# A gather kernel: index work by single batches in three steps, with TensorE and VectorE in program order

## The chip, the cores and the metric

One core of a Trainium2 chip. Times are device microseconds (us) of a whole execution. The runs of a kernel spread by 0.5 to 5%: those of the kernel before lie between 89.6 and 94.3 us over all their runs (one outlier of 171.8 left out as slow). A run more than 1.5% over the fastest of its kernel in the same set of runs counts as slow.

## The reference

```python
batch, seq, dim = 32, 512, 1024              # x: 32 x 512 x 1024 float32, indices: 32 x 128
for b in range(batch):
    result[b] = x[b, indices[b]]             # 128 rows of 4 KB per batch
```

Some of the 128 indices of a batch repeat. The kernel fetches each distinct row once, into a ring buffer, and spreads it to its places with a product by a 0/1 matrix.

## The kernel before

`HEAD` = 3 batches are fetched plainly. For the other 29, index work ("prep") finds the first user of each row (`junk`, `cnt`, `lead`), ranks the leaders by a product (`sm`, then `nth`, `slot`), packs row numbers by a second product (`pack`, `sm`, then `at`, `atF`) and makes the spreading matrix `s`. It is done for groups of two and then four batches.

```python
def prep(g0, g1):                                   # one group of up to four batches
    n, w = g1 - g0, slice(g0, g1)
    bc = pbc.tile([N, 4, N], F32, name="bc")        # PSUM, 2 buffers
    for b in range(g0, g1): nc.tensor.matmul(bc[:, b - g0], ...)
    for b in range(g0, g1): nc.vector.scalar_tensor_tensor(out=junk[:], in0=bc[:, b - g0], ..., accum_out=cnt[:, b:b + 1])
    nc.vector.tensor_scalar(out=lead16[:, w], ...); nc.vector.tensor_scalar(out=lead[:, w], ...)
    sm = psm.tile([N, B], F32, name="sm")           # PSUM, 2 buffers
    nc.tensor.matmul(sm[:, :n], lhsT=above[:], rhs=lead16[:, w], ...)
    # nth <- sm, nth ^= shift, slot <- nth: one VectorE operation each for the group
    for b in range(g0, g1):
        # pack <- turn, slot, lead
        last = nc.tensor.matmul(sm[:, 4 + b - g0:5 + b - g0], lhsT=pack[:], rhs=near[:, b:b + 1], ...)
    # at <- sm, atF <- sm: one each for the group
    for b in range(g0, g1): nc.vector.tensor_scalar(out=s[:], in0=bc[:, b - g0], scalar1=atF[:, b:b + 1], ...)
    return last
# ... cut
for b in range(HEAD, B):
    while done < len(groups) and groups[done][0] <= b + AHEAD:   # AHEAD = 8
        last = prep(*groups[done]); done += 1
    u = held[(b - HEAD) % RING]                                  # RING = 8
    gather(u, at[:, b:b + 1], b, bounds_check=S - 1, oob_is_err=False)
    ps = pout.tile([N, D], F32, name="ps")                       # PSUM, 2 buffers
    with tc.issue_after(last.ins):
        for h in range(2): nc.tensor.matmul(ps[:, h * 512:(h + 1) * 512], lhsT=spread[b][:], rhs=u[...], ...)
    if b < HEAD + 10:
        nc.scalar.copy(out=blocks[b][:], in_=ps[:])
    else:
        nc.vector.tensor_copy(out=blocks[b][:, :512], in_=ps[:, :512])
        nc.scalar.copy(out=blocks[b][:, 512:], in_=ps[:, 512:])
    nc.sync.dma_start(out=of[b * N:(b + 1) * N], in_=blocks[b][:])
```

Of the kernel before, what the change touches and what calls it, by code (L numbers as in the profile page):

```python
# [6 lines left out]
F32 = mybir.dt.float32  # L7
F16 = mybir.dt.float16
I32 = mybir.dt.int32
ALU = mybir.AluOpType  # L10


@with_exitstack
def kernel(ctx, tc, x, indices, out):
# [8 lines left out]



    nc = tc.nc
    B, S, D = x.shape
    N = indices.shape[1]
    HEAD, RING, FAR, AHEAD = 3, 8, 1024, 8
    assert S <= FAR  # L30
    const = ctx.enter_context(tc.tile_pool(name="const", bufs=1))
    ring = ctx.enter_context(tc.tile_pool(name="ring", bufs=1))
    rows = ctx.enter_context(tc.tile_pool(name="rows", bufs=1))
    pick = ctx.enter_context(tc.tile_pool(name="pick", bufs=1))
    junkp = ctx.enter_context(tc.tile_pool(name="junk", bufs=4))
    PS = bass.MemoryType.PSUM
    pbc = ctx.enter_context(tc.tile_pool(name="pbc", bufs=2, space=PS))
    psm = ctx.enter_context(tc.tile_pool(name="psm", bufs=2, space=PS))
    pout = ctx.enter_context(tc.tile_pool(name="pout", bufs=2, space=PS))


    first = const.tile([N, 1], indices.dtype, name="first")
    nc.sync.dma_start(out=first[:], in_=indices.rearrange("b n -> n b")[:, 0:1])
    v = const.tile([B, N], indices.dtype, name="v")
    nc.sync.dma_start(out=v[:], in_=indices)

    def low(t):
        return t[:].bitcast(I32).rearrange("p (n two) -> p n two", two=2)[:, :, 0]


    diff = const.tile([N, N], I32, name="diff")
    nc.gpsimd.iota(diff[:], pattern=[[1, N]], base=0, channel_multiplier=-1)
    rank = const.tile([N, 16, 8], I32, name="rank")
    for e in range(16):
        fold = 0
        for bit, col in enumerate((7, 5, 6, 3)):
            fold ^= col * (e >> bit & 1)
        steps = [[(-16 if fold >> bit & 1 else 16) << bit, 2] for bit in (2, 1, 0)]
        nc.gpsimd.iota(rank[:, e], pattern=steps, base=e + 16 * fold, channel_multiplier=0)  # L59
    shift = const.tile([N, 2, 16], I32, name="shift")  # L60
    nc.gpsimd.iota(shift[:], pattern=[[0, 2], [1, 16]], base=0, channel_multiplier=0)

    zero = const.tile([N, 1], F32, name="zero")
    nc.vector.memset(zero[:], 0.0)
    ident = const.tile([B, B], F16, name="ident")
    nc.vector.tensor_scalar(out=ident[:], in0=diff[:B, :B], scalar1=0, scalar2=None, op0=ALU.is_equal)
    below = const.tile([N, N], F16, name="below")
    nc.vector.tensor_scalar(out=below[:], in0=diff[:], scalar1=0, scalar2=None, op0=ALU.is_lt)
    above = const.tile([N, N], F16, name="above")
    turn = const.tile([N, N], F16, name="turn")  # L70
    nc.vector.tensor_copy(out=turn[:], in_=rank[:].rearrange("p e q -> p (e q)"))
    masks = nc.vector.tensor_scalar(out=above[:], in0=diff[:], scalar1=0, scalar2=None, op0=ALU.is_gt)
    vf = const.tile([B, N], F16, name="vf")
    with tc.issue_after(masks.ins):
        nc.vector.tensor_copy(out=vf[:], in_=low(v))  # L75


    tr = psm.tile([N, B], F32, name="sm")
    nc.tensor.matmul(tr[:], lhsT=vf[:], rhs=ident[:], start=True, stop=True)  # L79
    idxT = const.tile([N, B], I32, name="idxT")  # L80
    nc.vector.tensor_copy(out=idxT[:], in_=tr[:])
    idxF = const.tile([N, B], F32, name="idxF")
    nc.vector.tensor_copy(out=idxF[:], in_=tr[:])
    near = const.tile([N, B], F16, name="near")
    nc.vector.tensor_scalar(out=near[:], in0=tr[:], scalar1=float(-FAR), scalar2=None, op0=ALU.add)

    xf = x.flatten_outer_dims()
    of = out.flatten_outer_dims()

    def gather(dst, at, b, **kw):  # L90
        nc.gpsimd.indirect_dma_start(  # L91
            out=dst[:], out_offset=None,
            in_=xf[:], in_offset=bass.IndirectOffsetOnAxis(ap=at, axis=0),
            element_offset=b * S * D, **kw)

    blocks = [rows.tile([N, D], F32, name=f"block{b}") for b in range(B)]
    for b in range(HEAD):
        gather(blocks[b], first[:].bitcast(I32)[:, 0:1] if b == 0 else idxT[:, b:b + 1], b)
        nc.sync.dma_start(out=of[b * N:(b + 1) * N], in_=blocks[b][:])

    cnt = const.tile([N, B], F32, name="cnt")
    lead = const.tile([N, B], F32, name="lead")
    lead16 = const.tile([N, B], F16, name="lead16")
    nth = const.tile([N, B], I32, name="nth")
    slot = const.tile([N, B], F32, name="slot")
    atF = const.tile([N, B], F32, name="atF")
    at = const.tile([N, B], I32, name="at")
    spread = {}

    def prep(g0, g1):  # L110
        n, w = g1 - g0, slice(g0, g1)
        bc = pbc.tile([N, 4, N], F32, name="bc")
        for b in range(g0, g1):
            nc.tensor.matmul(bc[:, b - g0], lhsT=ident[:, b:b + 1].to_broadcast([B, N]),  # L114
                             rhs=vf[:], start=True, stop=True)
        for b in range(g0, g1):
            junk = junkp.tile([N, N], F16, name="junk")
            nc.vector.scalar_tensor_tensor(  # L118
                out=junk[:], in0=bc[:, b - g0], scalar=idxF[:, b:b + 1],
                in1=below[:], op0=ALU.is_equal, op1=ALU.mult, accum_out=cnt[:, b:b + 1])  # L120
        nc.vector.tensor_scalar(out=lead16[:, w], in0=cnt[:, w], scalar1=0.0, scalar2=None, op0=ALU.is_equal)  # L121
        nc.vector.tensor_scalar(out=lead[:, w], in0=cnt[:, w], scalar1=0.0, scalar2=None, op0=ALU.is_equal)  # L122
        sm = psm.tile([N, B], F32, name="sm")
        nc.tensor.matmul(sm[:, :n], lhsT=above[:], rhs=lead16[:, w], start=True, stop=True)  # L124
        nc.vector.tensor_copy(out=nth[:, w], in_=sm[:, :n])  # L125
        nc.vector.tensor_tensor(out=nth[:, w], in0=nth[:, w],  # L126
                                in1=shift[:].rearrange("p t s -> p (t s)")[:, w], op=ALU.bitwise_xor)
        nc.vector.tensor_copy(out=slot[:, w], in_=nth[:, w])  # L128
        for b in range(g0, g1):
            pack = junkp.tile([N, N], F16, name="pack")  # L130
            nc.vector.tensor_scalar(out=pack[:], in0=turn[:], scalar1=slot[:, b:b + 1],  # L131
                                    scalar2=lead[:, b:b + 1], op0=ALU.is_equal, op1=ALU.mult)
            last = nc.tensor.matmul(sm[:, 4 + b - g0:5 + b - g0], lhsT=pack[:], rhs=near[:, b:b + 1],  # L133
                                    start=True, stop=True)
        nc.vector.tensor_scalar(out=at[:, w], in0=sm[:, 4:4 + n], scalar1=float(FAR), scalar2=None, op0=ALU.add)  # L135
        nc.vector.tensor_scalar(out=atF[:, w], in0=sm[:, 4:4 + n], scalar1=float(FAR), scalar2=None, op0=ALU.add)
        for b in range(g0, g1):
            s = pick.tile([N, N], F32, name=f"s{b}")
            nc.vector.tensor_scalar(out=s[:], in0=bc[:, b - g0], scalar1=atF[:, b:b + 1],  # L139
                                    scalar2=None, op0=ALU.is_equal)  # L140
            spread[b] = s
        return last

    held = []
    for k in range(RING):
        u = ring.tile([N, D], F32, name=f"u{k}")
        nc.scalar.copy(out=u[:], in_=zero[:].to_broadcast([N, D]))  # L147
        held.append(u)

    groups = [(HEAD, HEAD + 2)] + [(g, min(g + 4, B)) for g in range(HEAD + 2, B, 4)]  # L150
    done = 0
    for b in range(HEAD, B):
        while done < len(groups) and groups[done][0] <= b + AHEAD:
            last = prep(*groups[done])
            done += 1
        u = held[(b - HEAD) % RING]
        gather(u, at[:, b:b + 1], b, bounds_check=S - 1, oob_is_err=False)
        ps = pout.tile([N, D], F32, name="ps")
        with tc.issue_after(last.ins):
            for h in range(2):  # L160
                nc.tensor.matmul(ps[:, h * 512:(h + 1) * 512], lhsT=spread[b][:],  # L161
                                 rhs=u[:, h * 512:(h + 1) * 512], start=True, stop=True)
        if b < HEAD + 10:
            nc.scalar.copy(out=blocks[b][:], in_=ps[:])  # L164
        else:
            nc.vector.tensor_copy(out=blocks[b][:, :512], in_=ps[:, :512])  # L166
            nc.scalar.copy(out=blocks[b][:, 512:], in_=ps[:, 512:])  # L167
        nc.sync.dma_start(out=of[b * N:(b + 1) * N], in_=blocks[b][:])


# [28 lines left out]
```

## Time and profile before

| kernel before | |
|---|---|
| median of 3 runs at the time of the prediction | 93.65 us (92.63 to 94.29) |
| span of the profiled run | 88.7 us (this run took 90.71 us, some 3 us under the median) |
| moved by the DMA | 31.98 MB |
| busy share: PE, DVE, ACT, POOL | 72%, 48%, 34%, 38% |

### The profile page before, as it was taken

The page shows a single profiled execution, that of the slowest core. Times are in us where ns is not written, and L with a number is a line of the kernel's source. Part 1 is how long each engine was busy: PE and PEld are TensorE (multiplying, and loading weights), DVE is VectorE, ACT ScalarE, POOL GpSimd, SP SyncE. Part 2 cuts the span into 40 slices and gives each one's busy share as a digit, 9 for nine tenths or more (in the row PEclk, how much of TensorE's full clock was granted, in tenths as well). Part 3 has the DMA queues.
Part 4 walks back from the last instruction along what each step waited for, and adds up shares of the span by engine and source line. Part 5 has one row for each costly group of instructions (what it writes and reads, how often), then busy time and mean ns, then how long its engine had stood idle before and what let it go on. Part 6 is the DMA issues. An engine that isn't in the chain of part 4 may idle for free.

```text
span 88.7 us, 852 instructions
## 1 busy us (share of the span) xinstructions
PE 63.5 (72%) x183; PEld 28.2 (32%) x183; DVE 42.5 (48%) x200; ACT 30.2 (34%) x38; POOL 33.9 (38%) x54
## 2 busy tenths in 40 slices
PE   0314225999997089999998079999999999992000
PEld 0303213344443043444443044344444434430000
DVE  1699999605002996005445994545735434533000
ACT  6999300044466001365223200223432342243000
POOL 7784778754456100366446100446544000000000
PEclk9999999999999995899999995799999999999955
DMA  0079898999999999999999999999999999999970
GB/s 0 15 214 264 340 316 320 421 419 418 414 419 423 421 419 414 412 390 414 395 421 416 405 421 429 395 244 384 395 399 416 419 414 425 419 417 421 414 310 6
DMA packets 9412, 31.98 MB, mean 360 GB/s; under 512 B 1589, under 2 KB 1621, under 8 KB 9408
## 3 DMA queue, kind: packets, MB, share of 16 engines
q1 hardware_dynamic: 4800, 16.81, 46.5%
q0 software_dynamic: 4608, 15.12, 45.7%
q14 instruction: 3, 0.02, 0.1%
q8 instruction: 1, 0.02, 0.1%
HBM read 16.81 MB, written 16.78 MB: 379 GB/s over the span
## 4 chain that ended last, share of the span: by engine, by line
PE 66%; DVE 13%; DMA 8%; POOL 2%; issue 2%; ACT 1%; POOLq 0%
PE ps L161 63%; DMA u<-in_x_dram,at 8%; DVE junk L118 6%; PE sm L133 2%; POOL rank L59 2%; DVE block L166 2%; DVE pack L131 1%; DVE lead L121 1%; ACT block L167 1%; DVE s L139 1%; DVE nth L125 0%; DVE lead L122 0%; PE bc L114 0%; DVE nth L126 0%; DVE slot L128 0%
## 5 line engine op out<-in xcount | busy, mean ns | idle before, releaser
L161 PE MATMUL ps<-u,s 128*128 128x512 f32 x116 | 56.5, 648 | 0.6 <-DMA u<-in_x_dram,at 0.6
L91 POOL DMA_INDIRECT u<-in_x_dram,at x29 | 28.7, 989 | 32.5 <-PE ps L161 25.6
L161 PEld LDWEIGHTS ps<-u,s 128*128 128x128 f32 x116 | 23.1, 207 | 29.5 <-issue 21.5
L166 DVE COPY block<-ps 128x512 f32<-128x512 f32 x19 | 13.1, 692 | 18.5 <-PE ps L161 17.4
L167 ACT COPY block<-ps 128x512 f32<-128x512 f32 x19 | 11.1, 585 | 28.6 <-DVE block L166 27.5
L164 ACT COPY block<-ps 128x1024 f32<-128x1024 f32 x10 | 10.1, 1012 | 22.1 <-PE ps L161 13.0
L118 DVE SCALAR_TENSOR_TENSOR junk<-bc,idxF,below 128x128 f16<-128x128 f32 x29 | 9.2, 345 | 6.1 <-PE bc L114 5.9
L139 DVE TENSOR_SCALAR s<-bc,atF 128x128 f32<-128x128 f32 x29 | 8.2, 344 | 0.1
L147 ACT COPY u<-zero 128x1024 f32<-128x1024 f32 x8 | 7.7, 1040 | 0.0
L131 DVE TENSOR_SCALAR pack<-turn,slot,lead 128x128 f16<-128x128 f16 x29 | 7.4, 334 | 0.6 <-DVE slot L128 0.5
L124 PE MATMUL sm<-lead,above 128*128 128x4 f16 (+2 forms) x8 | 1.4, 172 | 8.5 <-DVE lead L121 6.1
L135 DVE TENSOR_SCALAR at<-sm 128x4 int32<-128x4 f32 (+2 forms) x8 | 1.3, 162 | 10.4 <-PE sm L133 10.1
L114 PE MATMUL bc<-vf,ident 32*128 32x128 f16 x29 | 3.1, 255 | 2.6 <-DVE s L139 2.6
L133 PE MATMUL sm<-near,pack 128*128 128x1 f16 x29 | 3.5, 174 | 1.7 <-DVE pack L131 0.8
L133 PEld LDWEIGHTS <-pack 128*128 128x128 f16 x29 | 2.3, 99 | 7.2 <-DVE pack L131 3.7
L114 PEld LDWEIGHTS <-ident 32*128 32x128 f16 x29 | 2.2, 109 | 4.1 <-issue 4.1
L124 PEld LDWEIGHTS <-above 128*128 128x128 f16 x8 | 0.8, 100 | 7.2 <-issue 4.4
L79 PE MATMUL sm<-ident,vf 32*128 32x32 f16 x1 | 0.2, 204 | 3.4 <-DVE vf L75 3.4
L118 DVE DVE_READ_ACCUMULATOR junk<-bc,idxF,below 128x1 f32 x29 | 2.4, 83 | 0.0
L91 POOL DMA_INDIRECT block<-in_x_dram,idxT x2 | 1.9, 942 | 0.6 <-issue 0.6
L59 POOL IOTA rank<- 128x8 int32 x16 | 1.7, 141 | 0.0
L147 ACT ACT_TABLE_LOAD x1 | 1.3, 1283 | 0.7 <-PEq L183 0.7
(23 smaller groups left out, 11.6 us busy)
## 6 DMA issues: line engine op xcount, KB each, us to landing
out_dram<-block SPq DMA_DIRECT2D x32, 512.0 KB, 7.8
u<-in_x_dram,at POOLq DMA_INDIRECT x29
v<-in_indices_dram SPq DMA_DIRECT2D x1, 32.0 KB
block<-in_x_dram,idxT POOLq DMA_INDIRECT x2
first<-in_indices_dram SPq DMA_DIRECT2D x1, 1.0 KB, 1.8
block<-in_x_dram,first POOLq DMA_INDIRECT x1
```

Of the source, the lines that this page charges most:

```text
L59: nc.gpsimd.iota(rank[:, e], pattern=steps, base=e + 16 * fold, channel_multiplier=0)
L91: nc.gpsimd.indirect_dma_start(out=dst[:], out_offset=None, in_=xf[:], in_offset=bass.IndirectOffsetOnAxis(ap=at, axis=0), element_offset= ...
L114: nc.tensor.matmul(bc[:, b - g0], lhsT=ident[:, b:b + 1].to_broadcast([B, N]), rhs=vf[:], start=True, stop=True)
L118: nc.vector.scalar_tensor_tensor(out=junk[:], in0=bc[:, b - g0], scalar=idxF[:, b:b + 1], in1=below[:], op0=ALU.is_equal, op1=ALU.mult, ac ...
L131: nc.vector.tensor_scalar(out=pack[:], in0=turn[:], scalar1=slot[:, b:b + 1], scalar2=lead[:, b:b + 1], op0=ALU.is_equal, op1=ALU.mult)
L133: last = nc.tensor.matmul(sm[:, 4 + b - g0:5 + b - g0], lhsT=pack[:], rhs=near[:, b:b + 1], start=True, stop=True)
L139: nc.vector.tensor_scalar(out=s[:], in0=bc[:, b - g0], scalar1=atF[:, b:b + 1], scalar2=None, op0=ALU.is_equal)
L147: nc.scalar.copy(out=u[:], in_=zero[:].to_broadcast([N, D]))
L161: nc.tensor.matmul(ps[:, h * 512:(h + 1) * 512], lhsT=spread[b][:], rhs=u[:, h * 512:(h + 1) * 512], start=True, stop=True)
L164: nc.scalar.copy(out=blocks[b][:], in_=ps[:])
L166: nc.vector.tensor_copy(out=blocks[b][:, :512], in_=ps[:, :512])
L167: nc.scalar.copy(out=blocks[b][:, 512:], in_=ps[:, 512:])
```

## The change

Its intent: TensorE must no longer stop for the index work of a whole group. Index work goes by single batches, in three steps one round apart, so that each small product finds its input ready from the round before; TensorE and VectorE run in program order; all copies of the large product `ps` out of PSUM go to ScalarE, which frees VectorE; the constant table takes 8 iotas instead of 16.

```diff
-    HEAD, RING, FAR, AHEAD = 3, 8, 1024, 8
+    HEAD, RING, FAR, AHEAD = 3, 8, 1024, 9
+class InOrder:                     # each operation issued after the last one of its engine
+    ...
-    for e in range(16):            # rank: 16 iotas of 8
+    for e in range(8):             # rank: 8 iotas of 16
-    def prep(g0, g1): ...
+    def step0(b):
+        if b == HEAD or b % 4 == 0:
+            bcs["now"] = pbc.tile([N, 4, N], F32, name="bc")
+        bcs[b] = bc = bcs["now"][:, b % 4]
+        pe(mm, bc, ...)                                   # then junk/cnt, lead16, lead on VectorE
+    def step1(b):
+        if b == HEAD or b % 8 == 0:
+            sms["now"] = psm.tile([N, B], F32, name="sm")
+        sms[b] = sm = sms["now"][:, 2 * (b % 8):2 * (b % 8) + 2]
+        pe(mm, sm[:, 0:1], lhsT=above[:], rhs=lead16[:, col(b)], ...)   # then nth, xor, slot, pack
+    def step2(b):
+        pe(mm, sms[b][:, 1:2], lhsT=bcs[b, "pack"][:], rhs=near[:, col(b)], ...)  # then at, atF, s
+    def steps(t):
+        step0(t)
+        step2(t - 2)
+        step1(t - 1)
+    for t in range(HEAD, HEAD + AHEAD + 2):
+        steps(t)
+        if t - 2 < HEAD + RING:
+            fetch(t - 2)
     for b in range(HEAD, B):
-        ...
+        spread_rows(b)              # product, nc.scalar.copy of the whole ps, store
+        fetch(b + RING)
+        steps(b + AHEAD + 2)
```

More of the change, by code (lines that the diff above doesn't have):

```diff
@@ L10, with __init__, __call__ @@
 ALU = mybir.AluOpType
+class InOrder:
+    def __init__(self, tc):
+        self.tc, self.last = tc, None
+    def __call__(self, do, *args, **kw):
+        if self.last is None:
+            self.last = do(*args, **kw)
+        else:
+            with self.tc.issue_after(self.last.ins):
+                self.last = do(*args, **kw)
+        return self.last
 @with_exitstack
@@ L39 @@
     pout = ctx.enter_context(tc.tile_pool(name="pout", bufs=2, space=PS))
+    pe, dve = InOrder(tc), InOrder(tc)
+    mm, v = nc.tensor.matmul, nc.vector
     first = const.tile([N, 1], indices.dtype, name="first")
     nc.sync.dma_start(out=first[:], in_=indices.rearrange("b n -> n b")[:, 0:1])
-    v = const.tile([B, N], indices.dtype, name="v")
-    nc.sync.dma_start(out=v[:], in_=indices)
-    def low(t):
-        return t[:].bitcast(I32).rearrange("p (n two) -> p n two", two=2)[:, :, 0]
+    vals = const.tile([B, N], indices.dtype, name="vals")
@@ L51 @@
+    nc.sync.dma_start(out=vals[:], in_=indices)
     diff = const.tile([N, N], I32, name="diff")
     nc.gpsimd.iota(diff[:], pattern=[[1, N]], base=0, channel_multiplier=-1)
-    rank = const.tile([N, 16, 8], I32, name="rank")
-    for e in range(16):
+    rank = const.tile([N, 8, 16], I32, name="rank")
+    for e in range(8):
         fold = 0
-        for bit, col in enumerate((7, 5, 6, 3)):
+        for bit, col in enumerate((6, 5, 3)):
             fold ^= col * (e >> bit & 1)
         steps = [[(-16 if fold >> bit & 1 else 16) << bit, 2] for bit in (2, 1, 0)]
-        nc.gpsimd.iota(rank[:, e], pattern=steps, base=e + 16 * fold, channel_multiplier=0)
+        nc.gpsimd.iota(rank[:, e], pattern=[[1, 2]] + steps, base=2 * e + 16 * fold, channel_multiplier=0)
@@ L60 @@
     shift = const.tile([N, 2, 16], I32, name="shift")
     nc.gpsimd.iota(shift[:], pattern=[[0, 2], [1, 16]], base=0, channel_multiplier=0)
+    shift = shift[:].rearrange("p t s -> p (t s)")
     zero = const.tile([N, 1], F32, name="zero")
-    nc.vector.memset(zero[:], 0.0)
+    dve(v.memset, zero[:], 0.0)
     ident = const.tile([B, B], F16, name="ident")
-    nc.vector.tensor_scalar(out=ident[:], in0=diff[:B, :B], scalar1=0, scalar2=None, op0=ALU.is_equal)
+    dve(v.tensor_scalar, out=ident[:], in0=diff[:B, :B], scalar1=0, scalar2=None, op0=ALU.is_equal)
@@ L67 @@
     below = const.tile([N, N], F16, name="below")
-    nc.vector.tensor_scalar(out=below[:], in0=diff[:], scalar1=0, scalar2=None, op0=ALU.is_lt)
+    dve(v.tensor_scalar, out=below[:], in0=diff[:], scalar1=0, scalar2=None, op0=ALU.is_lt)
     above = const.tile([N, N], F16, name="above")
+    dve(v.tensor_scalar, out=above[:], in0=diff[:], scalar1=0, scalar2=None, op0=ALU.is_gt)
     turn = const.tile([N, N], F16, name="turn")
-    nc.vector.tensor_copy(out=turn[:], in_=rank[:].rearrange("p e q -> p (e q)"))
@@ L72 @@
-    masks = nc.vector.tensor_scalar(out=above[:], in0=diff[:], scalar1=0, scalar2=None, op0=ALU.is_gt)
+    dve(v.tensor_copy, out=turn[:], in_=rank[:].rearrange("p e q -> p (e q)"))
     vf = const.tile([B, N], F16, name="vf")
-    with tc.issue_after(masks.ins):
-        nc.vector.tensor_copy(out=vf[:], in_=low(v))
+    dve(v.tensor_copy, out=vf[:],
+        in_=vals[:].bitcast(I32).rearrange("p (n two) -> p n two", two=2)[:, :, 0])
     tr = psm.tile([N, B], F32, name="sm")
-    nc.tensor.matmul(tr[:], lhsT=vf[:], rhs=ident[:], start=True, stop=True)
+    pe(mm, tr[:], lhsT=vf[:], rhs=ident[:], start=True, stop=True)
@@ L80 @@
     idxT = const.tile([N, B], I32, name="idxT")
-    nc.vector.tensor_copy(out=idxT[:], in_=tr[:])
+    dve(v.tensor_copy, out=idxT[:], in_=tr[:])
     idxF = const.tile([N, B], F32, name="idxF")
-    nc.vector.tensor_copy(out=idxF[:], in_=tr[:])
+    dve(v.tensor_copy, out=idxF[:], in_=tr[:])
     near = const.tile([N, B], F16, name="near")
-    nc.vector.tensor_scalar(out=near[:], in0=tr[:], scalar1=float(-FAR), scalar2=None, op0=ALU.add)
+    dve(v.tensor_scalar, out=near[:], in0=tr[:], scalar1=float(-FAR), scalar2=None, op0=ALU.add)
@@ L94, in gather, with store @@
             element_offset=b * S * D, **kw)
+    def store(b):
+        nc.sync.dma_start(out=of[b * N:(b + 1) * N], in_=blocks[b][:])
     blocks = [rows.tile([N, D], F32, name=f"block{b}") for b in range(B)]
@@ L98 @@
         gather(blocks[b], first[:].bitcast(I32)[:, 0:1] if b == 0 else idxT[:, b:b + 1], b)
-        nc.sync.dma_start(out=of[b * N:(b + 1) * N], in_=blocks[b][:])
-    cnt = const.tile([N, B], F32, name="cnt")
-    lead = const.tile([N, B], F32, name="lead")
-    lead16 = const.tile([N, B], F16, name="lead16")
-    nth = const.tile([N, B], I32, name="nth")
-    slot = const.tile([N, B], F32, name="slot")
-    atF = const.tile([N, B], F32, name="atF")
-    at = const.tile([N, B], I32, name="at")
@@ L108 @@
-    spread = {}
-    def prep(g0, g1):
-        n, w = g1 - g0, slice(g0, g1)
-        bc = pbc.tile([N, 4, N], F32, name="bc")
-        for b in range(g0, g1):
-            nc.tensor.matmul(bc[:, b - g0], lhsT=ident[:, b:b + 1].to_broadcast([B, N]),
-                             rhs=vf[:], start=True, stop=True)
-        for b in range(g0, g1):
-            junk = junkp.tile([N, N], F16, name="junk")
-            nc.vector.scalar_tensor_tensor(
-                out=junk[:], in0=bc[:, b - g0], scalar=idxF[:, b:b + 1],
-                in1=below[:], op0=ALU.is_equal, op1=ALU.mult, accum_out=cnt[:, b:b + 1])
-        nc.vector.tensor_scalar(out=lead16[:, w], in0=cnt[:, w], scalar1=0.0, scalar2=None, op0=ALU.is_equal)
-        nc.vector.tensor_scalar(out=lead[:, w], in0=cnt[:, w], scalar1=0.0, scalar2=None, op0=ALU.is_equal)
-        sm = psm.tile([N, B], F32, name="sm")
-        nc.tensor.matmul(sm[:, :n], lhsT=above[:], rhs=lead16[:, w], start=True, stop=True)
-        nc.vector.tensor_copy(out=nth[:, w], in_=sm[:, :n])
-        nc.vector.tensor_tensor(out=nth[:, w], in0=nth[:, w],
-                                in1=shift[:].rearrange("p t s -> p (t s)")[:, w], op=ALU.bitwise_xor)
-        nc.vector.tensor_copy(out=slot[:, w], in_=nth[:, w])
-        for b in range(g0, g1):
-            pack = junkp.tile([N, N], F16, name="pack")
-            nc.vector.tensor_scalar(out=pack[:], in0=turn[:], scalar1=slot[:, b:b + 1],
-                                    scalar2=lead[:, b:b + 1], op0=ALU.is_equal, op1=ALU.mult)
-            last = nc.tensor.matmul(sm[:, 4 + b - g0:5 + b - g0], lhsT=pack[:], rhs=near[:, b:b + 1],
-                                    start=True, stop=True)
-        nc.vector.tensor_scalar(out=at[:, w], in0=sm[:, 4:4 + n], scalar1=float(FAR), scalar2=None, op0=ALU.add)
-        nc.vector.tensor_scalar(out=atF[:, w], in0=sm[:, 4:4 + n], scalar1=float(FAR), scalar2=None, op0=ALU.add)
-        for b in range(g0, g1):
-            s = pick.tile([N, N], F32, name=f"s{b}")
-            nc.vector.tensor_scalar(out=s[:], in0=bc[:, b - g0], scalar1=atF[:, b:b + 1],
-                                    scalar2=None, op0=ALU.is_equal)
-            spread[b] = s
-        return last
@@ new lines, with table, col @@
+        store(b)
+    def table(name, dtype):
+        return const.tile([N, B], dtype, name=name)
+    cnt, lead, slot, atF = table("cnt", F32), table("lead", F32), table("slot", F32), table("atF", F32)
+    lead16, nth, at = table("lead16", F16), table("nth", I32), table("at", I32)
+    bcs, sms, spread = {}, {}, {}
+    def col(b):
+        return slice(b, b + 1)
+    def step0(b):
+        if not HEAD <= b < B:
+            return
+        if b == HEAD or b % 4 == 0:
+            bcs["now"] = pbc.tile([N, 4, N], F32, name="bc")
+        bcs[b] = bc = bcs["now"][:, b % 4]
+        pe(mm, bc, lhsT=ident[:, col(b)].to_broadcast([B, N]), rhs=vf[:], start=True, stop=True)
+        junk = junkp.tile([N, N], F16, name="junk")
+        dve(v.scalar_tensor_tensor, out=junk[:], in0=bc, scalar=idxF[:, col(b)], in1=below[:],
+            op0=ALU.is_equal, op1=ALU.mult, accum_out=cnt[:, col(b)])
+        dve(v.tensor_scalar, out=lead16[:, col(b)], in0=cnt[:, col(b)], scalar1=0.0, scalar2=None,
+            op0=ALU.is_equal)
+        dve(v.tensor_scalar, out=lead[:, col(b)], in0=cnt[:, col(b)], scalar1=0.0, scalar2=None,
+            op0=ALU.is_equal)
@@ new lines, in step1 @@
+    def step1(b):
+        if not HEAD <= b < B:
+            return
+        if b == HEAD or b % 8 == 0:
+            sms["now"] = psm.tile([N, B], F32, name="sm")
+        sms[b] = sm = sms["now"][:, 2 * (b % 8):2 * (b % 8) + 2]
+        pe(mm, sm[:, 0:1], lhsT=above[:], rhs=lead16[:, col(b)], start=True, stop=True)
+        dve(v.tensor_copy, out=nth[:, col(b)], in_=sm[:, 0:1])
+        dve(v.tensor_tensor, out=nth[:, col(b)], in0=nth[:, col(b)], in1=shift[:, col(b)],
+            op=ALU.bitwise_xor)
+        dve(v.tensor_copy, out=slot[:, col(b)], in_=nth[:, col(b)])
+        pack = junkp.tile([N, N], F16, name="pack")
+        dve(v.tensor_scalar, out=pack[:], in0=turn[:], scalar1=slot[:, col(b)],
+            scalar2=lead[:, col(b)], op0=ALU.is_equal, op1=ALU.mult)
+        bcs[b, "pack"] = pack
@@ new lines, in step2 @@
+    def step2(b):
+        if not HEAD <= b < B:
+            return
+        pe(mm, sms[b][:, 1:2], lhsT=bcs[b, "pack"][:], rhs=near[:, col(b)], start=True, stop=True)
+        dve(v.tensor_scalar, out=at[:, col(b)], in0=sms[b][:, 1:2], scalar1=float(FAR), scalar2=None,
+            op0=ALU.add)
+        dve(v.tensor_scalar, out=atF[:, col(b)], in0=sms[b][:, 1:2], scalar1=float(FAR), scalar2=None,
+            op0=ALU.add)
+        spread[b] = s = pick.tile([N, N], F32, name=f"s{b}")
+        dve(v.tensor_scalar, out=s[:], in0=bcs[b], scalar1=atF[:, col(b)], scalar2=None,
+            op0=ALU.is_equal)
@@ L144, with fetch @@
+    def fetch(b):
+        if HEAD <= b < B:
+            gather(held[(b - HEAD) % RING], at[:, col(b)], b, bounds_check=S - 1, oob_is_err=False)
+    def steps(t):
+        step0(t)
+        step2(t - 2)
+        step1(t - 1)
     held = []
@@ L148, with spread_rows @@
         held.append(u)
-    groups = [(HEAD, HEAD + 2)] + [(g, min(g + 4, B)) for g in range(HEAD + 2, B, 4)]
-    done = 0
-    for b in range(HEAD, B):
-        while done < len(groups) and groups[done][0] <= b + AHEAD:
-            last = prep(*groups[done])
-            done += 1
-        u = held[(b - HEAD) % RING]
-        gather(u, at[:, b:b + 1], b, bounds_check=S - 1, oob_is_err=False)
-        ps = pout.tile([N, D], F32, name="ps")
-        with tc.issue_after(last.ins):
-            for h in range(2):
-                nc.tensor.matmul(ps[:, h * 512:(h + 1) * 512], lhsT=spread[b][:],
-                                 rhs=u[:, h * 512:(h + 1) * 512], start=True, stop=True)
-        if b < HEAD + 10:
-            nc.scalar.copy(out=blocks[b][:], in_=ps[:])
-        else:
-            nc.vector.tensor_copy(out=blocks[b][:, :512], in_=ps[:, :512])
-            nc.scalar.copy(out=blocks[b][:, 512:], in_=ps[:, 512:])
-        nc.sync.dma_start(out=of[b * N:(b + 1) * N], in_=blocks[b][:])
+    def spread_rows(b):
+        ps = pout.tile([N, D], F32, name="ps")
+        for h in range(2):
+            pe(mm, ps[:, h * 512:(h + 1) * 512], lhsT=spread[b][:],
+               rhs=held[(b - HEAD) % RING][:, h * 512:(h + 1) * 512], start=True, stop=True)
+        nc.scalar.copy(out=blocks[b][:], in_=ps[:])
+        store(b)
+    for t in range(HEAD, HEAD + AHEAD + 2):
+        steps(t)
+        if t - 2 < HEAD + RING:
+            fetch(t - 2)
+    for b in range(HEAD, B):
+        spread_rows(b)
+        fetch(b + RING)
+        steps(b + AHEAD + 2)
 _INS = ['x', 'indices']
```

## The prediction

> **What bounds the kernel now.** I first read the page's 40 slices (one slice is 2.2 us), because the kernel moves 32 MB and the question is whether the transfers ever starve.
>
> ```profile
> PE   0314225999997089999998079999999999992000
> DVE  1699999605002996005445994545735434533000
> DMA  0079898999999999999999999999999999999970
> GB/s 0 15 214 264 340 316 320 421 419 418 414 419 423 421 419 414 412 390 414 395 421 416 405 421 429 395 244 384 395 399 416 419 414 425 419 417 421 414 310 6
> ```
>
> From slice 7 on the 16 DMA engines are full at about 418 GB/s. 31.98 MB at 418 GB/s is 76.5 us of an 88.7 us span. So the bound is the DMA, and the rest is where it starves. TensorE (PE), which carries 63% of the page's chain, has gaps at slices 12-13 and 21-22 and ends long before the DMA does: it is a feeder, not the bound. To size the starving I asked for stretches (busy us of PE, weight loads, DVE, ACT, POOL; clock; DMA share; GB/s last).
>
> ```profile
> 4.00:16.00 12.00, 4.37 (x26) 2.56 (x24) 11.34 (x74) 5.69 (x7) 8.28 (x10) 1.00 0.86 286
> 16.00:36.00 20.00, 17.27 (x48) 7.68 (x47) 8.59 (x50) 7.00 (x7) 8.36 (x9) 0.92 1.03 418
> 36.00:56.00 20.00, 16.93 (x50) 7.23 (x50) 10.00 (x47) 5.46 (x8) 7.58 (x9) 0.93 1.02 410
> 56.00:66.00 10.00, 10.00 (x27) 4.30 (x25) 5.04 (x13) 3.33 (x6) 5.42 (x6) 0.96 1.00 359
> 66.00:84.00 18.00, 14.28 (x34) 5.80 (x32) 6.23 (x9) 5.45 (x10) 1.07 (x2) 1.00 1.03 420
> ```
>
> Against 418 GB/s the head (4 to 16 us) loses 12 x 132/418 = 3.8 us, 36 to 56 loses 0.4 us, 56 to 66 loses 1.4 us. Everything else is full. What feeds it is the order of gathers on POOL:
>
> ```profile
> 7.93 1.00 POOL L91 DMA_INDIRECT u<-in_x_dram,at  x1 [1.28 <-DVE slot L128]
> 9.23 0.99 POOL L91 DMA_INDIRECT u<-in_x_dram,at  x1 [0.30 <-issue]
> ...
> 17.00 1.05 POOL L91 DMA_INDIRECT u<-in_x_dram,at  x1 [0.30 <-issue]
> 19.04 0.99 POOL L91 DMA_INDIRECT u<-in_x_dram,at  x1 [0.99 <-issue]
> ...
> 28.08 0.98 POOL L91 DMA_INDIRECT u<-in_x_dram,at  x1 [0.73 <-PE ps L161]
> 35.30 0.98 POOL L91 DMA_INDIRECT u<-in_x_dram,at  x1 [6.24 <-PE ps L161]
> ```
>
> The first eight ring gathers leave at 7.93 to 17.00, 1.3 us apart, POOL's own pace. Then each waits for a `ps` product to free its buffer. TensorE stops at 28-32 and 48-52 us for the index work of a whole group, so no gather leaves for 7 us. The queue hides most of this; the dip at 56-66 us is what reaches the DMA.
>
> **What the Trainium skill says.**
> 1. "VectorE: DVE Perf Modes", section "The DRAIN you can't avoid": a semaphore between VectorE operations costs nothing extra, though a read after a write on the engine needs one. The trace differs for these small tiles. Independent small operations start 0.07 to 0.08 us apart, a dependent pair 0.19 us apart (the write must end, then 0.035 us):
>
> ```profile
> 52.19 0.16 DVE L126 TENSOR_TENSOR nth<-nth,shift 128x3 int32<-128x3 int32 x1
> 52.38 0.17 DVE L128 CAST slot<-nth 128x3 f32<-128x3 int32 x1
> 52.55 0.17 DVE L135 TENSOR_SCALAR at<-sm 128x4 int32<-128x4 f32 x1
> 52.63 0.15 DVE L136 TENSOR_SCALAR atF<-sm 128x4 f32<-128x4 f32 x1
> ```
>
> 2. "TensorE: Matmul & The Clock Gate", Part 1: the array starts at half rate and needs a busy window of about 3.4 us, free-running, to reach full rate. The trace agrees: passes of the first `ps` start 0.86 us apart (16.00, 16.85, 17.71), and from 19.30 on 0.43 us apart.
> 3. "DMA: Bandwidth & Descriptors", section "Bandwidth": a fabric ceiling of 435 GB/s. The trace shows 418 to 420 in full stretches, so no faster steady state is to be had; only starving can be won back.
>
> **The change, part by part.**
>
> *Constants.* Eight iotas go from POOL. The 16 took 1.70 us, 0.105 apart; eight of double length save about 0.8 us. The first gather then waits only for its indices, whose last piece landed at 2.5 us, so it leaves at about 2.55, not 3.04. `vf` waits for the other index load (landed 2.84) and moves only from 3.06 to 2.9, so the first `junk` starts at 3.85, not 4.00. The first ring gather leaves once POOL is free, at about 6.5 instead of 7.93.
>
> *Index work.* Bytes, products and gathers stay the same. Seven small VectorE operations that served a group of up to four (8 of each) now run once per batch (29 of each), and the fixed program order keeps the scheduler from filling their waits with other batches' `junk`. One step costs, start to start:
>
> - `junk` 0.27, then `lead16` after the accumulator read 0.12, `lead` 0.07, `at` 0.07, `atF` 0.08: 0.61
> - `s` waits for `atF`: 0.19; `s` itself 0.27 until `nth` starts: 0.46
> - `nth` to `xor`, `xor` to `slot`, `slot` to `pack`, all dependent: 3 x 0.19 = 0.58
> - `pack` until the next `junk`: 0.23
>
> Sum 1.88 us per batch. Before, DVE finished ten batches' index work (and part of the next four) between 4.0 and 15.7 us, under 1.2 us per batch.
>
> *The opening.* TensorE now runs eleven steps (batches 3 to 13) in order ahead of the first product. Step 3 is 0.53 us, step 4 is 1.34, steps 5 to 12 are 8 x 1.88 = 15.0: VectorE ends at 3.85 + 16.9 = 20.8, and after the two small products on the last `pack` and `lead16` the first `ps` starts at about 21.2 us, where it is now 14.99. The ring gathers leave at 6.5, 8.3, then 1.88 apart, the eighth at 19.6 (now 17.0). Their data (8 x 0.467 MB, from 15.12 MB of the gather queue less 3 whole blocks of 0.524, over 29), the 3 whole blocks and their 3 stores are 6.9 MB and are through at about 23. The first `ps` runs cold, 4 x 0.86 = 3.44 us, to 24.7; only then can the ninth gather leave, and its data comes about 1.8 us later (from the trace: issue at 3.04, first bytes near 4.9), at 26.6. The first store of a product needs a 1.01 us ScalarE copy and 2 us to first bytes, so about 27.8. The DMA lies empty for 3.5 us or so. At 26.6 us the kernel before has moved 7.88 MB (sum of the GB/s over 2 us stretches); the changed one 6.88 MB. That is 1.0 MB/418 GB/s = 2.4 us behind, and about 0.6 us more while the queues refill.
>
> *Steady state.* One batch of TensorE is 4 x 0.43 = 1.72 plus some 0.25 for three small products, about 2.0 us; VectorE's 1.88 fits under it. Each batch releases 0.99 MB, which takes the DMA 2.36 us. So once going, the DMA stays full, and the 0.4 + 1.4 us of stretches 36-66 (with a little at 48-56) come back: about 1.9 us.
>
> *Copies.* From batch 13 on, a copy was half on DVE (0.69) then half on ACT (0.58), one after the other, 1.28 us; one ACT copy is 1.01 us. [...]This frees 13.1 us of DVE, but two PSUM buffers and a 1.72 us product hide it both before and after: nothing on the path.
>
> Sum: +2.4 + 0.6 - 1.9 = +1.1 us, nearly all set by the opening. The DMA would end near 87.3 instead of 86.2, and 93.65 becomes 94.7.
>
> **Rivals.**
> - *The opening costs nothing and the smooth middle wins.* For it: earlier first gathers by 1.4 us, and no TensorE stall. It would hold if a step took 1.5 us, as when the dependent waits are overlapped: 8 x 0.38 = 3 us sooner, 91.7 us. Against: the dependent pairs in the trace are all 0.19 us.
> - *The loop becomes bound by TensorE and VectorE ordering each other.* If `pack` of one step comes late for TensorE's program order, a batch takes 2.5 us instead of 2.0: the 18 batches with index work would then feed less than 418 GB/s and the end moves by 2 to 3 us: 97. Against: bc, packs and products are spread over different steps, so that each has a whole step of slack.
> - *Warm-up falls worse.* The free-running window may keep the second product cold as well: +1 to 2 us. Or TensorE is warm from the small products, -1.7 us; it was not before, with denser small products.
> - *Index permutation unbalances the 16 DMA engines.* The new table still leaves one empty place per eight neighbouring rows; I see no cost.
>
> **Range and chances.** A step wrong by 0.13 us moves the end by 1 us, the warm-up by 1 to 2 us, and the three times of before spread by 1.7 us. The balance of two effects near 2 us each leaves "same" likeliest, leaning slow. Since the opening looks worse and the steady rate can't rise, a gain over 2% needs the step time to be badly off. Range 92.2 to 97.0; faster 0.13, same 0.55, slower 0.32.
>
> **What would show it.** First `ps` at about 21 us (step time: successive `at` 1.9 us apart); GB/s near zero around 23 to 26 us; first ring gather near 6.5; 418 GB/s from 30 us to the end with no dip near 58; no half-clock after the first warm-up; first products 3.4 us. If `ps` starts before 18 us, my step cost is wrong and the change wins; if the rate from 30 us on stays under 400, the loop is bound by its own order.

## The result, and the profile after

| | median, us | runs | ratio of fast runs to fast runs of before | 95% interval |
|---|---|---|---|---|
| before | 93.71 | 4 (92.63 to 94.29) | | |
| after | 105.47 | 4 (104.14 to 107.11) | 1.117 | 1.099 to 1.135 |

Ratios here and below are the mean time of one kernel's fast runs over that of the other's of the same rounds, so not quite the ratio of the medians quoted. Two of the four runs of after, 106.52 and 107.11, count as slow; its fast ones took 104.14 and 104.42. The change made the kernel 12% slower; the prediction had +1% and a range up to 97.0. The profiled run of after is a fast one (104.14 us, span 102.2).

The slices of after, on the page (2.56 us each):

```profile
PE   0233323369777977887777978977778999999600
DVE  2589989880665585556655585566555400000000
DMA  1289899994399999999899999999999999999990
GB/s 12 25 292 316 303 372 417 422 366 184 26 335 292 306 324 367 365 335 335 317 329 325 309 335 369 365 354 346 340 313 309 340 332 375 390 423 420 410 383 37
```

There are two things to see. At slices 9 and 10 (23 to 28 us) the DMA runs dry, as predicted. And from slice 11 to 33 the rate stays near 335 GB/s instead of 418, which the prediction had only as a rival. The DMA row shows nines all the same: it is no sign of a full DMA.

The stretches of after, in the same columns as those of before in the prediction:

```profile
4.00:16.00 12.00, 3.39 (x18) 1.39 (x18) 10.82 (x75) 5.69 (x7) 6.88 (x7) 1.00 0.88 301
16.00:36.00 20.00, 13.95 (x41) 5.36 (x41) 12.49 (x82) 4.05 (x4) 6.95 (x7) 1.00 0.84 291
36.00:56.00 20.00, 14.97 (x47) 5.52 (x46) 11.87 (x76) 7.08 (x7) 6.77 (x7) 1.00 0.99 337
56.00:66.00 10.00, 8.56 (x26) 3.23 (x25) 6.17 (x38) 3.04 (x3) 3.17 (x4) 1.00 0.99 343
66.00:84.00 18.00, 14.78 (x44) 6.13 (x44) 8.82 (x54) 7.09 (x7) 6.96 (x7) 1.00 0.99 335
```

Between 36 and 56 us TensorE is busy 14.97 of 20 us and VectorE 11.87: neither is full, and the DMA's 337 GB/s is 0.81 of the 418 that the kernel before has in its full stretches. Somebody waits for somebody, every round.

The gathers of after on POOL, with the idle time before each:

```profile
7.69 1.00 POOL L109 DMA_INDIRECT u<-in_x_dram,at  x1 [1.25 <-DVE nth L24]
9.50 1.00 POOL L109 DMA_INDIRECT u<-in_x_dram,at  x1 [0.81 <-DVE nth L24]
...
20.45 0.99 POOL L109 DMA_INDIRECT u<-in_x_dram,at  x1 [0.83 <-DVE nth L24]
25.70 0.99 POOL L109 DMA_INDIRECT u<-in_x_dram,at  x1 [4.25 <-PE bc L24]
...
34.82 0.99 POOL L109 DMA_INDIRECT u<-in_x_dram,at  x1 [2.05 <-PE sm L24]
36.94 0.99 POOL L109 DMA_INDIRECT u<-in_x_dram,at  x1 [1.12 <-PE sm L24]
```

The opening is much as worked out: ring gathers 1.82 us apart (predicted 1.88), the first at 7.69 (6.5), the eighth at 20.45 (19.6), the ninth at 25.70 (24.8). After that a round takes 3.04 us, 16 times; only twice it takes 2.12, at 36.94 and 60.35. Those two belong to the rounds in which the rank product is that of batch 16 and batch 24, and `b % 8 == 0` is where the changed kernel takes a new `sm` tile. So the long rounds should come from sharing that tile. One long round, all engines in order of time:

```profile
51.81 0.23 PE L24 MATMUL bc<-vf,ident 32*128 32x128 f16 x1
51.97 0.18 PE L24 MATMUL sm<-near,pack 128*128 128x1 f16 x1
...
52.60 0.15 DVE L24 TENSOR_SCALAR at<-sm 128x1 int32<-128x1 f32 x1
52.66 0.15 DVE L24 TENSOR_SCALAR atF<-sm 128x1 f32<-128x1 f32 x1
...
52.86 0.16 PE L24 MATMUL sm<-lead,above 128*128 128x1 f16 x1 [0.72 <-DVE atF L24]
...
52.97 1.95 PE L24 MATMUL ps<-u,s 128*128 128x512 f32 x4
```

and the round ahead of 36.94, of TensorE alone:

```profile
34.64 0.18 PE L24 MATMUL sm<-near,pack 128*128 128x1 f16 x1
34.68 0.16 PE L24 MATMUL sm<-lead,above 128*128 128x1 f16 x1
34.70 1.96 PE L24 MATMUL ps<-u,s 128*128 128x512 f32 x4
```

In the long round the rank product (`sm<-lead,above`) of one batch waits 0.72 us until `atF` of the batch before it has been read, although it uses another column. Ahead of `at` stand `junk` and both `lead` of this round on VectorE. The next big product stands behind the rank product on TensorE. In the short round the rank product follows within 0.04 us. A round of 3.04 us releases 0.99 MB, which is 326 GB/s: about the rate of the slices.

The Trainium skill gives a reason for such a wait, on a page that the prediction does not name: "PSUM — Partial Sum Buffer", section "PSUM bank collisions raise a hardware error", says that two engines on the same bank and partitions collide even at different columns, and gives the rule: "Semaphore-guard PSUM by **bank × quadrant** (by bank is the simple version), not by address." This trace agrees in so far as there is such a wait, 0.72 us long; that the bank is what matters is the page's word. The runs show only that several batches in one tile make the wait, since none of them separates tile from bank.

One view spoke for another cause. Of the waits of after (total us, times, longest):

```profile
PE sm L24 <- DVE atF L24: 15.4, 25, 0.7
PEld ps L24 <- ACT block L198: 14.8, 23, 0.9
```

The second line says that the big products waited for the ScalarE copies of the change just as long. Both can't be the cause; the experiments had to tell.

### The profile page after: what moved, and what is told of

It reads as the page before. It is cut to its first block, busy times and chain, and to the rows that moved or that the text cites. A ratio compares the mean times of both kernels' runs of the same rounds, so it can differ in the third digit from the quotient of the medians.

```text
span 102.2 us, 1015 instructions
## 1 busy us (share of the span) xinstructions
PE 68.4 (67%) x204; PEld 27.0 (26%) x204; DVE 51.3 (50%) x328; ACT 38.3 (37%) x38; POOL 33.6 (33%) x46
## 3 DMA queue, kind: packets, MB, share of 16 engines
q0 software_dynamic: 4608, 15.12, 48.4%
## 4 chain that ended last, share of the span: by engine, by line
PE 60%; DVE 28%; issue 3%; DMA 2%; ACT 1%; SPq 0%; DVEq 0%
PE ps L24 54%; DVE junk L24 9%; DVE lead L24 6%; PE sm L24 3%; PE bc L24 3%; DVE pack L24 3%; DVE s L24 3%; DVE nth L24 2%; DMA vals<-in_indices_dram 2%; DVE atF L24 2%; DVE at L24 2%; DVE slot L24 1%; ACT block L198 1%; SPq L63 0%; DVE vf L24 0%
## 5 line engine op out<-in xcount | busy, mean ns | idle before, releaser
L198 ACT COPY block<-ps 128x1024 f32<-128x1024 f32 x29 | 29.4, 1012 | 58.3 <-PE ps L24 54.9
L24 PEld LDWEIGHTS ps<-u,s 128*128 128x128 f32 x116 | 20.8, 194 | 33.2 <-issue 18.4
L24 PE MATMUL sm<-lead,above 128*128 128x1 f16 x29 | 4.7, 163 | 16.2 <-DVE atF L24 15.4
L24 PE MATMUL bc<-vf,ident 32*128 32x128 f16 x29 | 6.9, 246 | 0.7 <-DVE s L24 0.4
L24 DVE TENSOR_SCALAR lead<-cnt 128x1 f16<-128x1 f32 (+1 forms) x58 | 6.2, 150 | 1.0
L24 DVE TENSOR_SCALAR at<-sm 128x1 int32<-128x1 f32 x29 | 4.3, 149 | 2.0 <-PE sm L24 2.0
L24 DVE TENSOR_TENSOR nth<-nth,shift 128x1 int32<-128x1 int32 x29 | 4.7, 161 | 1.1
L24 DVE CAST slot<-nth 128x1 f32<-128x1 int32 x29 | 4.5, 154 | 1.0
L24 DVE TENSOR_SCALAR atF<-sm 128x1 f32<-128x1 f32 x29 | 4.3, 148 | 0.0
L24 DVE CAST nth<-sm 128x1 int32<-128x1 f32 x29 | 4.3, 148 | 0.0
```

The costliest lines, as they stand in the source:

```text
L24: self.last = do(*args, **kw)
```

## The experiments

Theory A: the wait on the shared small PSUM tile costs 0.92 us a round and is the loss that the prediction missed; what is left without it is the predicted opening. Theory B: the products wait for the whole copies on ScalarE.

| run | us, median | ratio | 95% interval |
|---|---|---|---|
| e1 two small tiles | 94.24 | 1.015 | 1.002 to 1.027 |
| e2 position step first | 105.34 | 1.122 | 1.103 to 1.140 |
| e3 one small tile for all | 107.75 | 1.161 | 1.151 to 1.172 |
| e4 before, copies on ScalarE | 91.50 | 0.986 | 0.970 to 1.001 |
| e5 e1 with grouped opening | 88.86 | 0.957 | 0.943 to 0.970 |
| e6 at, atF first, s late | 98.38 | 1.062 | 1.045 to 1.079 |
| e7 e1, five ahead | 91.95 | 0.978 | 0.955 to 1.000 |
| e8 e4 and eight iotas | 92.36 | none | |
| e9 e5 with the shared tile | 98.80 | none | |
| e10 e5 again, 5 rounds | 88.91 | 0.987 | 0.976 to 0.998 |
| e11 e4 again, 5 rounds | 92.25 | none | |

All gave correct results. Ratios are to the kernel before on the same chip. In this table they leave out the profiled run of each kernel and judge a run as fast against the fastest of those that remain; three runs have none, for want of enough fast runs.

**e1.** Even and odd batches keep their small results in two tiles.

```diff
-        if b == HEAD or b % 8 == 0:
-            sms["now"] = psm.tile([N, B], F32, name="sm")
-        sms[b] = sm = sms["now"][:, 2 * (b % 8):2 * (b % 8) + 2]
+        if ("now", b % 2) not in sms:
+            sms["now", b % 2] = psm.tile([N, B], F32, name="sm")
+        sms[b] = sm = sms["now", b % 2][:, 2 * (b // 2):2 * (b // 2) + 2]
```

> The changed kernel with one edit: even and odd batches keep their small PSUM results (rank and position) in two different tiles instead of one tile shared by up to eight batches. Theory A: in the changed kernel the rank product of one batch waits for the position read (atF) of the batch before only because both lie in one tile; without that a batch takes about 2.1 us on TensorE instead of 3.04 us, the DMA becomes the bound again and only the slow opening of the prediction is left: about 95 us (94 to 97). Theory B (the waits view puts 14.8 us of weight loads down to the ScalarE copy of the product before): the products wait for the ScalarE copies; then nothing changes, about 105 us and still 3.0 us per batch.

Measured 94.24 us. A round of e1 on TensorE, then a line of its waits view, then a ScalarE copy with the product that follows it, then two of its stretches:

```profile
30.12 0.18 PE L24 MATMUL sm<-near,pack 128*128 128x1 f16 x1
30.16 0.16 PE L24 MATMUL sm<-lead,above 128*128 128x1 f16 x1
30.19 1.96 PE L24 MATMUL ps<-u,s 128*128 128x512 f32 x4
```

```profile
PEld ps L24 <- ACT block L198: 1.9, 6, 0.7
```

```profile
53.35 1.01 ACT L198 COPY block<-ps 128x1024 f32<-128x1024 f32 x1 [1.10 <-PE ps L24]
53.47 1.53 PE L24 MATMUL ps<-u,s 128*128 128x512 f32 x3
```

```profile
22.00:30.00 8.00, 8.00 (x19) 2.71 (x17) 4.13 (x26) 2.02 (x2) 2.00 (x2) 1.00 0.65 205
36.00:56.00 20.00, 20.00 (x68) 7.76 (x68) 16.43 (x103) 9.65 (x10) 9.29 (x10) 1.00 1.02 403
```

The wait is gone, each round takes 2.12 us, and the DMA is back at 403. The copies are as they were in the changed kernel, and the 14.8 us of waits put down to them fell to 1.9: theory B falls. In e1 a product starts at 53.47, while the copy of the product before it runs from 53.35 to 54.36; in after such a copy had merely ended at about the moment when the rank product let TensorE go on (52.93 in the round above). What is left against the kernel before is 1.5% by the ratio, and 3.0% against the two runs that count as fast when the profiled one is kept (90.75 and 92.09). The stretch of 205 GB/s at 22 to 30 us shows where it is lost.

**e2.** The position step ahead of the count step: `step2(t - 2); step0(t); step1(t - 1)`.

> The changed kernel with the position step ahead of the count step in each round, so VectorE does at and atF first and the shared-tile wait is shorter by about 0.55 us but not gone. Theory A: about 2.5 us per batch instead of 3.04, 16 batches x 0.55 = 9 us saved, about 96.5 us (95 to 98.5). Theory B: unchanged, about 105 us.

Measured 105.34: the expectation missed. Its trace, of a run that counts as slow, shows why, in the waits of TensorE:

```profile
53.70 0.21 PE L24 MATMUL bc<-vf,ident 32*128 32x128 f16 x1 [0.73 <-DVE s L24]
```

Now `s`, which reads the broadcast `bc` of an earlier batch, comes ahead of the next `bc` product, and four batches share one `bc` tile: the same kind of wait on the other shared tile. It also stretched the opening: the ninth gather left at 30.46 instead of 25.70, and the second product ran cold as well (3.76 us where after has 1.96). So e2 says nothing on the size of the first wait.

**e3.** One tile of 64 columns for all batches.

> The changed kernel with a single small PSUM tile for all batches, so that the two batches (16 and 24) which now start a fresh tile and take 2.1 us lose that. Theory A: two batches more at 3.04 us, +1.8 us, about 107 us and no short period left in the gathers. Theory B: unchanged, about 105 us, short periods stay.

Measured 107.75, 2.3 us over the median of after and 3.4 over its fast runs; no short round is left in the gathers. The size is muddied: in the trace of e3 the second product ran cold, that is, at about half its pace (3.60 us where after has 1.96). Its 1.6 us and the two rounds, 2 x 0.92, would make up the 3.4.

**e4.** The kernel before with `nc.scalar.copy(out=blocks[b][:], in_=ps[:])` for every batch.

> The kernel before with all PSUM copies whole on ScalarE, nothing else of the change. Theory A and the prediction: the copies lie beside the products, same time as before within 1% (93.7 us). Theory B: products would wait for the 1.01 us copies, some 18 x 0.9 us of TensorE time, so clearly slower, over 97 us.

Measured 91.50, no slower. In this kernel the whole copies on ScalarE cost nothing that the interval shows.

**e5.** As e1, but batches 3 to 12 are prepared in groups of two, four and four, by the code of `prep` above and in the scheduler's order; single steps begin with batch 13.

```diff
-    for t in range(HEAD, HEAD + AHEAD + 2):
-        steps(t)
-        if t - 2 < HEAD + RING:
-            fetch(t - 2)
+    FIRST = HEAD + AHEAD + 1
+    for g0, g1 in ((HEAD, HEAD + 2), (HEAD + 2, HEAD + 6), (HEAD + 6, FIRST)):
+        opening(g0, g1)
+        for b in range(g0, min(g1, HEAD + RING)):
+            fetch(b)
+    step0(FIRST)
```

> The two-tile version (run e1) with batches 3 to 12 prepared at the start in groups of two, four and four as in the kernel before (left to the scheduler's own order), then single steps as in e1. Theory A (what is left of the loss in e1 is the opening: 1.83 us per batch of VectorE steps ahead of the first product): first product at about 14.5 us instead of 21.7, no empty DMA near 22 to 26 us, 2.12 us per batch after it, the DMA full from 16 us to the end: about 91 to 92 us, 2 us under the kernel before. Rival (single steps in TensorE's program order cost the loop itself, opening hidden): within 1% of e1, 94 us.

Measured 88.86, better than expected and faster than every run of either kernel. The first product starts at 15.79 us (21.08 in e1). The same two stretches in e5:

```profile
22.00:30.00 8.00, 8.00 (x29) 2.99 (x27) 6.59 (x42) 3.58 (x5) 3.62 (x4) 1.00 1.03 420
36.00:56.00 20.00, 20.00 (x69) 7.86 (x69) 16.45 (x105) 9.85 (x10) 9.46 (x10) 1.00 1.03 417
```

So the rest of the loss was the opening, and beyond that the single-step loop does what the change was meant to do: no dip anywhere after 18 us.

**e6.** The changed kernel (shared small tile) with `at` and `atF` first, then the count step, then `s`, then the rank step, so that `bc` waits for nothing.

> Mends what spoiled e2 (there the broadcast product waited for s of an earlier batch in the same four-batch bc tile, 0.73 us in its trace): the changed kernel, one shared small tile as in it, with at and atF first, then the count step, then s, then the rank step. Theory A (a wait by tile, as long as VectorE takes to reach atF): about 2.55 us per batch, between 3.04 (changed) and 2.12 (e1), about 97 us (95.5 to 99.5). If the wait were not for atF: 3.04 us and 105 us.

Measured 98.38, with rounds of 2.41 us (2.55 expected). The rank product now waits 0.19 us for `atF`, not 0.72. The round grows with how long VectorE takes to reach `atF`: 2.12 without the wait, 2.41 and 3.04 with it. The opening was slower (gathers 2.2 us apart, the ninth at 28.64), which may be why the total was not lower; no run separates the two.

**e7.** e1 with `AHEAD = 5`, and `steps`, `fetch(b + AHEAD)`, `spread_rows(b)` in this order in each round.

> The two-tile version (run e1) working five batches ahead instead of nine, the index step and the gather put in front of the product in each round. Theory A on the opening: the first product no longer stands behind eleven steps but seven, so it starts about 4 x 1.83 = 7.3 us sooner, near 14.4 us; gathers go on at 2.1 us or less; about 91.5 us (90 to 93). Rival (nine ahead is needed to cover the gathers' 7 us): products wait for gathers, over 94 us.

Measured 91.95. The first product starts at 15.91 us, not 14.4: with the step ahead of the product in each round, eight steps stand before it and not seven (the last small products of the eighth are at 15.49 and 15.54), and then it waits 0.21 us for its gather. Both sides of the expectation have a part: the opening shrinks, but 22 to 30 us still has 292 GB/s, and later products wait for gathers (0.96 us before the one at 42.12). The profiled run counts as slow, so these times are only a sketch.

**e8.** e4 with the eight iotas of the change.

> The kernel before with two parts of the change alone: all PSUM copies whole on ScalarE (run e4) and eight iotas in place of sixteen. By the prediction the iotas let the first gather go 0.5 us sooner and the first index work 0.15 us sooner: 0.2 to 0.5 us under e4 (91.5), so about 91.2 us; not told apart from e4 by the interval, but the first gather should leave near 2.7 us instead of 3.04.

Measured 92.36, without a ratio: only its fastest run, of 90.51, counts as fast. The first gather left at 2.75 us instead of 3.04; an effect of this size is not seen in the total.

**e9.** e5 with the shared tile put back.

> The grouped opening of run e5 with the changed kernel's shared small tile put back in the loop: the fourth corner of opening x tile. Theory A: with 3.04 us per batch the loop is bound by TensorE, so the whole 5.9 us by which the first product starts sooner (15.8 against 21.7) comes off the changed kernel's 105.5: about 99.5 us (98 to 101), and 3.04 us per batch in the gathers. If the opening only mattered through an empty DMA that a slow loop hides, it would stay near 105.

Median 98.80, with 3.04 us rounds again in its profiled (slow) run, but its only fast run took 95.90 and the three others count as slow. It fits the fourth corner in direction (the tile costs some 7 to 10 us also with the good opening); a size is not to be had from it.

**e10 and e11.** e5 and e4 once more.

> Run e5 once more, unchanged, for a tighter interval: 88.9 us, 4 to 5% under the kernel before. If the gain was chance of one chip, within 2% of it.

> Run e4 once more, unchanged, because its interval left it open (0.970 to 1.001). The prediction says the copies are off the path: within 1% of the kernel before. In the trace of e4 the second group's index work starts 0.4 us sooner after the last product because no half copy on VectorE stands before it: at most 0.5 us.

e10: 88.91 us, six runs within 88.53 to 89.37, but the ratio is 0.987, not 0.957: the kernel before had two fast runs beside these runs, of 89.61 and 90.71, and nine that count as slow. Each of the ten runs of this version is faster than every run of the kernel before. By the two ratios the gain is 1.3 or 4.4%, and their intervals reach from 0.2 to 5.7%; where in them it lies stays open. e11: 92.25, where the kernel before has 92.27, without a ratio: the copies change nothing that can be told from noise.

## Why the prediction was wrong

- **The bound.** Right: the DMA, and what feeds it. e5 shows that a full DMA is what a better feeder gives.
- **The opening.** Right in mechanism, a little small in size: steps of 1.83 us on VectorE (predicted 1.88), first product at 21.66 (21.2), ninth gather at 25.70 (24.8), and 0 GB/s from 25.5 to 27.0 us (predicted: empty from about 23 to 26.6). The first ring gather was to leave at 6.5, once POOL is free; it left at 7.69, about 0.96 us after the start of the `at` that it needs, as in the kernel before (6.98 to 7.93). The first `junk` came at 4.18, not 3.85.
- **A sum that agrees in part by luck.** With the missed wait removed (e1), the kernel takes 94.24 us, where the prediction said 94.7. But its sums were read from a run of 90.71 us and added to a median of 93.65. Profile against profile, e1's span is 3.6 us longer, not 1.1: over the first 36 us it moves 274 GB/s and before 329, which is 1.98 MB or 4.7 us behind (2.4 + 0.6 predicted), and what comes back after that is 1.1 us (1.9 predicted). Part of it is the rival on warm-up: the second product of e1 took 2.85 us instead of 1.96. In after it did not (1.96).
- **Steady state: the step that failed.** "One batch of TensorE is 4 x 0.43 = 1.72 plus some 0.25 for three small products, about 2.0 us" measured 3.04. Of the excess, 0.12 is that the products cost 2.12 in all (e1), and 0.92 is the wait of the rank product for `atF` of the batch before in the same PSUM tile. 16 rounds x 0.92 = 14.7 us of TensorE; the last product starts at 94 rather than 81 us. The end moves by less, 9.9 us between the spans of e1 and after, because in e1 the DMA and no longer TensorE set the end; by the prediction's own 2.36 us of DMA per batch one would estimate 16 x (3.04 - 2.36) = 10.9 us. The "about 1.9 us" that the smooth middle was to give back therefore never came: 36 to 56 us went from 410 to 337 GB/s.
- **The rival on order.** The prediction named a loop bound by TensorE and VectorE ordering each other, at 2.5 us and 97 us, and set it aside because every input is ready a step earlier. That was true of the data. The order came from a PSUM tile that several batches share; the prediction never asked who writes into `sm` while who reads from it. Grouped work did not meet this: each group has a small tile of its own, and its second products need what the read of the rank gives anyway. The loss also takes program order, in which the big product stands behind the rank product; a run with the two the other way round was not made.
- **Copies.** "Nothing on the path": consistent with e4 and e11, in so far as their spread lets one tell.
- **Iotas.** The eight took 1.26 us, so 0.44 us was saved and not 0.8. The first gather gained 0.26 us instead of 0.5, since it then waited 0.36 us for its index load; no effect in the total was seen.
- **What would show it.** "If the rate from 30 us on stays under 400, the loop is bound by its own order" was the line that came true. No half-clock after the first warm-up came true too: 36 to 84 us of after show a clock of 1.00, where before had 0.92 to 0.96 in three of its stretches.

## What to carry to other kernels

When work is split into finer pieces in program order, list for every PSUM tile which pieces write it and which read it, and see whether a write of one piece now falls between reads of another: several batches in one tile make them wait for each other even at different columns. Alternating two tiles changed three lines and gave back some 10 us (fast runs of 104.3 to 94.2). And a pipeline by single items pays its fixed costs per item before the first result: open with groups and go over to single steps when the queue is full, which is the version that beat both kernels.

## What the Trainium skill lacked or had wrong

- "VectorE: DVE Perf Modes", section "The DRAIN you can't avoid", has a semaphore between VectorE operations cost nothing extra, measured on eight larger copies (13.88 us either way). With tiles this small a dependent pair started 0.19 us apart and an independent one 0.07 to 0.08, the semaphore and the wait for the result not being told apart; such pairs help to make the step of 1.83 us in the changed kernel.
- "PSUM — Partial Sum Buffer", section "PSUM bank collisions raise a hardware error", has the rule but not its price in a pipeline: here 0.72 us of waiting and 0.92 us of a 3.04 us round, because the read that is waited for stands behind other work on its engine.
- "Perfetto Trace Analysis", section "Identifying the Most-Contended Engine", warns that DMA occupancy misleads and is right: 0.99 busy at 337 GB/s in after, 1.03 at 417 in e5. It doesn't say that the same packets can take longer in a slower run: those of the gather queue took 48.4% of a span of 102.2 us in after (49.5 us) and 45.7% of 88.7 us before (40.5 us), for the same 15.12 MB.
- "DMA: Bandwidth & Descriptors", section "Anatomy of one DMA — SWDGE (gpsimd) path", calls descriptor generation small and variable and gives no figure for an indirect gather. One of 128 rows held POOL for 1.0 us here, and gathers left at best 1.3 us apart, which set the pace of the first eight ring gathers of the kernel before (7.93 to 17.00 us).
